# A decoder trunk on one core: seven products per weight pair in the first FFN too, with the first transposition of h behind the up projection, later weight sums, and seven raw and eleven split buffers

## The chip, the cores and the metric

The kernel runs on one core of one Trainium2 chip. The time is the device time of one execution in microseconds (us); three executions of the kernel before took 991.8 to 993.68 us, with a median of 992.76 us. One execution was taken by the hardware profiler, and all rows below come from it. Engines are named as in the profile: PE multiplies matrices, DVE is the vector engine, ACT the scalar engine, POOL the general one, and SP issues the DMAs.

## The reference

Two layers work on x, 256 tokens of 1024 channels, in float32. Each layer is a half-step SwiGLU FFN, a token mixer and a second FFN, each followed by a layer norm:

```python
def swiglu(x, w_gate, w_up, w_down):
    return (jax.nn.silu(x @ w_gate) * (x @ w_up)) @ w_down
...
for l in range(DEPTH):
    x = layer_norm(ALPHA * x + 0.5 * swiglu(x, ffn1_gate[l], ffn1_up[l], ffn1_down[l]), ...)
    # three mixers on x @ w_in[l] (short convolution, gated MLP, sparse attention), then w_out[l]
    x = layer_norm(ALPHA * x + mix, ...)
    x = layer_norm(ALPHA * x + 0.5 * swiglu(x, ffn2_gate[l], ffn2_up[l], ffn2_down[l]), ...)
```

An FFN has 2816 hidden channels: gate and up are 1024 x 2816, down is 2816 x 1024. There are four FFNs; below they are called FFN 1 to 4 in order of time, with the mixer of layer 0 between FFN 1 and FFN 2 and that of layer 1 between FFN 3 and FFN 4.

## The kernel before

Weights arrive in DRAM order as blocks of 128 x 1024 floats (512 KB) through one stream of DMAs on SP, into a pool of raw buffers. Every block is split into two parts of a shorter float format: ACT casts raw to `hi`, DVE computes `lo` = raw - hi, and a product of two split operands is three matmuls (hi*hi, lo*hi, hi*lo: `mm3`, L246 to L250, and `proj_chan`, L258 to L260). A raw buffer comes free when both parts are made; `hi` and `lo` come free when PE has used them. There are 5 raw, 12 hi and 12 lo buffers.

An FFN (`ffn`, L390) goes through the hidden channels in ten chunks, the first of 512, the others of 256. In the first chunk the tokens are the stationary side: PE makes gate and up of token half 0 and then of half 1 (`tok`; tiles pg, pu, each 24 matmuls of 512 columns). `gated` is the Silu on ACT (tile sg), `product` multiplies on DVE (tile h), and `trans` transposes h on PE (tile tr), from where it is split to hTh and hTl. The two halves use the same two PSUM banks in turn (`gu_bank`): the gate of half 1 takes the bank of the gate of half 0, and the up projection of half 1 takes the bank of the up projection of half 0, which the product h of half 0 reads. Only in FFN 1 do the gates lie in other banks, so that there the two up projections have a bank each. In the chunks after that the weights are the stationary side (`chan`, 48 matmuls of 256 columns for gate and as many for up).

The down projection of the first six chunks is done in two ways. `_paired` gives 0 for FFN 1: there `down` multiplies every block of 128 hidden channels with both token halves and both halves of the output, 4 products of three matmuls of 512 columns. In the other three FFNs two blocks form a pair and a scheme of seven products in place of eight is used (`paired`, tiles M1 to M7). It has its price on ACT and DVE: `pair_operands` makes sums of the pair's raw weights in place (L202, four of 128 x 512 a pair) and splits them, `left_sums` does the same with h (tile S), and `combine` adds the seven results to x. The split of two of the weight sums is a closure, `rest`, that waits in `put_off` until more blocks were loaded. A pair's two raw buffers are held until `rest` has run. Seven pairs fall into the first six chunks. During these chunks gate and up of one chunk share a single bank (tag `free`), so the up projection cannot start before the Silu has read the gate. The bank `held` is kept for M3.

The framework orders the instructions of each engine itself, from the program's order, priorities and its own estimate of times; each engine then works strictly in that order. `ensure` puts loads and splits 7 blocks ahead of their use.

Of the kernel before, what the change touches and what calls it, by code (L numbers as in the profile page):

```python
# [31 lines left out]

def _paired(l, f):

    return 0 if (l, f) == (0, 1) else 6


def _w_in_groups():  # L40
# [92 lines left out]
def _build(tc, A, out):  # L133
# [3 lines left out]
    with ExitStack() as es:  # L137
        pool = lambda name, bufs, **k: es.enter_context(tc.tile_pool(name=name, bufs=bufs, **k))
        cst = pool("cst", 1)
        rawp = pool("raw", 5)  # L140
        hip = pool("hi", 12)
        lop = pool("lo", 12)
        wk = pool("wk", 9)
        sm = pool("sm", 3)
        lnp = pool("lnp", 1)
# [3 lines left out]
        def gu_bank(shape, name):  # L149
            turns.append(1)  # L150
            return ps.tile(shape, F32, name=name, tag=f"gu{len(turns) % 2}", bufs=1)
# [9 lines left out]
        loaded = []  # L161
# [3 lines left out]
        put_off = []  # L165

        def ensure(i):
            while len(loaded) <= min(i, len(plan) - 1):
                key, k, n, split, o = plan[len(loaded)]
                src = A["ws"][o:o + 128 * n].rearrange("(p c) -> p c", p=128)  # L170
                if len(key) == 4 and key[2] == "d" and key[3] < _paired(*key[:2]):
                    raw = rawp.tile([128, n], F32, name="raw", tag="raw")
                    stream.append(SP.dma_start(raw, src))
                    if k % 2 == 0:
                        loaded.append(raw)
                    else:
                        loaded[-1], rest = pair_operands(loaded[-1], raw)
                        loaded.append(loaded[-1])
                        put_off.append((len(loaded), rest))
                    continue  # L180
                if not split:
                    raw = (hip, lop)[k % 2].tile([128, n], F32, name="w1", tag=("hi", "lo")[k % 2])
                    SP.dma_start(raw, src)
                    loaded.append((raw, None))
                    continue
                raw = rawp.tile([128, n], F32, name="raw", tag="raw")
                stream.append(SP.dma_start(raw, src))
                hi = hip.tile([128, n], F32R, name="hi", tag="hi")
                lo = lop.tile([128, n], F32R, name="lo", tag="lo")
                splits.append((ACT.copy(hi, raw),  # L190
                               DVE.tensor_tensor(lo, raw, hi.bitcast(F32), ALU.subtract)))  # L191
                loaded.append((hi, lo))
                while put_off and put_off[0][0] < len(loaded) - 1:
                    put_off.pop(0)[1]()

        def pair_operands(ra, rb):
# [39 lines left out]
        def kslices(key, n, ahead=None):  # L236

            res = []
            for hi, lo in blocks(key, ahead):
                m = hi.shape[1] // n  # L240
                res += [(hi[:, i * n:(i + 1) * n], lo[:, i * n:(i + 1) * n]) for i in range(m)]
            return res
# [3 lines left out]
        def mm3(o, a, b, start, stop):  # L246

            PE.matmul(o, lhsT=a[0], rhs=b[0], start=start, stop=False)  # L248
            PE.matmul(o, lhsT=a[0], rhs=b[1], start=False, stop=False)  # L249
            return PE.matmul(o, lhsT=a[1], rhs=b[0], start=False, stop=stop)  # L250
# [34 lines left out]
        def xT(t, k):  # L285
            c = slice(t * 128, t * 128 + 128)
            return xTh[:, k, c], xTl[:, k, c]
# [101 lines left out]

        def ffn(l, f, lni, last=False, mid=None):  # L390
            n = len(CHUNKS)
            paired_chunks = _paired(l, f)
            late = 4
            y = {}
            started = set()
# [2 lines left out]
            def tok(name, t, in_y=False, ahead=None):  # L398

                w = kslices((l, f, name, 0), 512, ahead)  # L400
                if in_y:
                    p = ps.tile([128, 512], F32, name="p" + name, tag="y", bufs=4)
                else:
                    p = gu_bank([128, 512], "p" + name)
                products[:] = [mm3(p, xT(t, k), w[k], k == 0, k == KC - 1) for k in range(KC)]
                return p
# [17 lines left out]
            def product(p, sg):  # L424
                h = wk.tile([128, 512], F32, name="h", tag="w")
                DVE.tensor_tensor(h, p.rearrange("p a b -> p (a b)") if len(p.shape) == 3 else p, sg, ALU.mult)  # L426
                return h
# [3 lines left out]
            def hpair():  # L431
                return (wk.tile([128, 512], F32R, name="hTh", tag="a"),
                        wk.tile([128, 512], F32R, name="hTl", tag="a"))

            def trans(h, t):
                tr = ps.tile([128, 512], F32, name="tr", tag="tr")
                for i in range(4):
                    c = slice(i * 128, i * 128 + 128)
                    PE.transpose(tr[:, c], h[:, c], ident)
                hT[0, t] = hpair()  # L440
                if paired_chunks:
                    hf[t] = wk.tile([128, 4, 128], F32, name="hf", tag="w")
                    ACT.copy(hf[t].rearrange("p a b -> p (a b)"), tr)
                    tr = hf[t].rearrange("p a b -> p (a b)")
                split_to(*hT[0, t], tr)
# [30 lines left out]
            def paired(c, ms):  # L476

                for m in ms:
                    if m not in M:
                        tag, bufs = {3: (held, 1), 6: ("tr", 2), 7: ("tr", 2)}.get(m, ("y", 4))  # L480
                        M[m] = ps.tile([128, 512], F32, name=f"M{m}", tag=tag, bufs=bufs)
                    for i in range(CHUNKS[c][1] // 256):
                        w = blocks((l, f, "d", c))[2 * i]
                        mm3(M[m], left_side(c, i, m), w[m], c == 0 and i == 0,
                            c == paired_chunks - 1 and i == CHUNKS[c][1] // 256 - 1)
# [36 lines left out]
            h = {}  # L522
            if l == 0 and f == 1:
                sg = [gated(tok("g", 0, True, ahead=0))]
                with ExitStack() as order:
                    for i in second_x(products):
                        order.enter_context(tc.issue_after(i.ins))
                    ensure(index[l, f, "g", 0][-1] + 3)
                sg.append(gated(tok("g", 1, True)))
                h = {t: product(tok("u", t), sg[t]) for t in range(2)}  # L530
                trans(h[0], 0)
            else:
                for t in range(2):
                    sg = gated(tok("g", t))
                    if t == 1:
                        trans(h[0], 0)
                    h[t] = product(tok("u", t), sg)

            if paired_chunks:
                turns.append(1)  # L540
                free, held = f"gu{len(turns) % 2}", f"gu{1 - len(turns) % 2}"
            for c in range(1, n):
                p = chan("g", c)
                with tc.high_priority(offset=60):
                    sg = gated(p)
                if c == 1:
                    trans(h[1], 1)
                if c <= paired_chunks:
                    if c == 1:
                        for i in range(2):  # L550
                            a = lambda t, b: hf[t][:, 2 * i + b, :]
                            left_sums(0, i, a(0, 0), a(0, 1), a(1, 0), a(1, 1))
                    paired(c - 1, (1, 2, 4, 5))
                elif not paired_chunks:
                    if c > 1 and c - 2 < n - late:
                        down([c - 2], 1)
                    if c - 1 < n - late:
                        down([c - 1], 0)
                pu = chan("u", c)
                with tc.high_priority(offset=60):  # L560
                    hc = product(pu, sg)
                if c <= paired_chunks:
                    paired(c - 1, (6, 7, 3))
                hT[c] = hpair()
                split_to(*hT[c], hc)
                if c < paired_chunks:
                    a = lambda t, b: hc[:, b * 256 + t * 128:b * 256 + t * 128 + 128]
                    left_sums(c, 0, a(0, 0), a(0, 1), a(1, 0), a(1, 1))
                if c == paired_chunks:
                    combine()  # L570
                if c == 2:
                    with tc.issue_after(stream[-1].ins):
                        gb = load_ln(l, lni)
                if c == 4 and mid:
                    with tc.issue_after(stream[-1].ins):
                        mid()
# [362 lines left out]
```

## Time and profile before

| | us |
|---|---|
| median of three executions | 992.76 |
| lowest, highest | 991.8, 993.68 |
| the profiled execution | 994.34 |
| its span, first to last instruction | 992.6 |
| PE, DVE, ACT busy | 969.1, 734.8, 512.3 |

The span is a little shorter than the execution, since launch and end lie outside it. Busy shares are taken over the whole span. Because the ends of matmuls are modelled, PE's pace is read from start to start of neighbouring matmuls rather than from its busy time.

### The profile page before, as it was taken

What the parts mean: (1) busy time and instruction counts of PE and PEld (TensorE: products, weight loads), DVE (VectorE), ACT (ScalarE), POOL (GpSimd) and SP (SyncE); (2) the same over time, 40 slices, a digit from 0 to 9 for tenths busy, and PEclk for the clock granted to TensorE, in tenths of its full rate; (3) what the DMA queues carried; (4) which work ended last, traced back from release to release, by engine and by line L of the source; (5) the groups of instructions that cost most, each with busy time, mean ns of one, the idle gap of its engine ahead of it and who ended that gap; (6) DMA issues with size and microseconds to landing.
All of it is one profiled execution on the core that took longest, in us unless ns stands there. A gap on an engine that the chain in (4) does not pass through costs nothing.

```text
span 992.6 us, 16879 instructions
## 1 busy us (share of the span) xinstructions
PE 969.1 (98%) x6765; PEld 875.8 (88%) x6765; DVE 734.8 (74%) x1094; ACT 512.3 (52%) x730; POOL 19.8 (2%) x42
## 2 busy tenths in 40 slices
PE   7999999999999999999999999999999999999996
PEld 5899999899878799999879899998988778989995
DVE  5755454586869978877598888848678797888844
ACT  6644444256556655555255556534475555556520
POOL 1000000010000000000000000000000000000000
PEclk9999999999999999999999999999999999999999
DMA  7977566284323557677245667764742245757611
GB/s 256 344 237 226 181 194 193 96 324 147 111 86 128 179 180 236 194 253 233 86 151 171 233 214 253 237 200 148 256 149 80 84 158 170 253 196 232 213 60 43
DMA packets 53069, 183.19 MB, mean 185 GB/s; under 512 B 6656, under 2 KB 7168, under 8 KB 52992
## 3 DMA queue, kind: packets, MB, share of 16 engines
q1 hardware_dynamic: 52992, 182.12, 55.0%
q8 instruction: 53, 0.87, 0.4%
q14 instruction: 24, 0.20, 0.1%
HBM read 181.05 MB, written 1.05 MB: 183 GB/s over the span
## 4 chain that ended last, share of the span: by engine, by line
PE 74%; DVE 11%; DMA 9%; issue 3%; ACT 3%; SPq 0%; DVEq 0%; ACTq 0%
DMA raw<-in_ws 8%; PE pu L258 6%; PE pu L260 6%; PE pu L259 6%; PE pg L258 5%; PE pg L260 5%; PE pg L259 5%; PE y L248 4%; PE y L250 4%; PE y L249 4%; DVE raw L202 3%; PE pc L258 3%; PE pc L260 3%; PE pc L259 3%; DVE lo L263 3%
## 5 line engine op out<-in xcount | busy, mean ns | idle before, releaser
L191 DVE TENSOR_TENSOR lo<-raw,hi 128x1024 fp32r<-128x1024 f32 (+3 forms) x284 | 336.6, 1200 | 115.2 <-ACT hi L190 113.5
L190 ACT CAST hi<-raw 128x1024 fp32r<-128x1024 f32 (+3 forms) x284 | 289.8, 1034 | 247.4 <-PE pu L259 64.7
L258 PE MATMUL pu<-xTh,hi 128*128 128x256 f32 x576 | 161.7, 281 | 3.4 <-ACT sg L421 3.4
L258 PE MATMUL pg<-xTh,hi 128*128 128x256 f32 x576 | 161.6, 281 | 0.5 <-DVE h L426 0.5
L260 PE MATMUL pu<-xTh,lo 128*128 128x256 f32 x576 | 160.9, 279 | 0.0
L260 PE MATMUL pg<-xTh,lo 128*128 128x256 f32 x576 | 160.8, 279 | 0.0
L259 PE MATMUL pu<-xTl,hi 128*128 128x256 f32 x576 | 160.8, 279 | 0.0
L259 PE MATMUL pg<-xTl,hi 128*128 128x256 f32 x576 | 160.8, 279 | 0.0
L258 PEld LDWEIGHTS pu<-xTh,hi 128*128 128x128 f32 x576 | 108.0, 188 | 7.1 <-ACT sg L421 5.9
L263 ACT CAST hi<-raw 128x1024 fp32r<-128x1024 f32 x63 | 66.2, 1052 | 90.5 <-DVE raw L202 46.5
L258 PEld LDWEIGHTS pg<-xTh,hi 128*128 128x128 f32 x576 | 108.1, 188 | 2.3 <-DVE h L426 1.2
L259 PEld LDWEIGHTS pu<-xTl,hi 128*128 128x128 f32 x576 | 107.9, 187 | 1.2
L260 PEld LDWEIGHTS pu<-xTh,lo 128*128 128x128 f32 x576 | 108.2, 188 | 0.2
L259 PEld LDWEIGHTS pg<-xTl,hi 128*128 128x128 f32 x576 | 107.9, 187 | 0.5
L260 PEld LDWEIGHTS pg<-xTh,lo 128*128 128x128 f32 x576 | 108.2, 188 | 0.0
L263 DVE TENSOR_TENSOR lo<-raw,hi 128x1024 fp32r<-128x1024 f32 x63 | 76.7, 1219 | 30.6 <-ACT hi L263 21.7
L258 PE MATMUL pc<-xTh,hi 128*128 128x256 f32 x256 | 73.0, 285 | 0.5 <-DVE kd L630 0.5
L248 PE MATMUL y<-hi,hTh 128*128 128x512 f32 x184 | 72.4, 394 | 0.0
L260 PE MATMUL pc<-xTh,lo 128*128 128x256 f32 x256 | 72.4, 283 | 0.0
L259 PE MATMUL pc<-xTl,hi 128*128 128x256 f32 x256 | 71.8, 281 | 0.0
L250 PE MATMUL y<-hi,hTl 128*128 128x512 f32 x184 | 71.8, 390 | 0.0
L249 PE MATMUL y<-lo,hTh 128*128 128x512 f32 x184 | 71.6, 389 | 0.0
(188 smaller groups left out, 1702.0 us busy)
## 6 DMA issues: line engine op xcount, KB each, us to landing
raw<-in_ws SPq DMA_DIRECT2D x312, 512.0 KB, 4.6
w<-in_ws SPq DMA_DIRECT2D x8, 512.0 KB, 6.2
lng<-in_ln SPq DMA_DIRECT2D x6, 512.0 KB, 6.8
lnb<-in_ln SPq DMA_DIRECT2D x6, 512.0 KB, 7.7
raw<-in_ws SPq DMA_DIRECT2D x8, 256.0 KB, 4.8
raw<-in_ws SPq DMA_DIRECT2D x4, 420.0 KB, 4.3
x<-in_x SPq DMA_DIRECT2D x4, 256.0 KB, 5.6
out<-x SPq DMA_DIRECT2D x4, 256.0 KB, 2.1
```

The source lines that it names most:

```text
L190: splits.append((ACT.copy(hi, raw), DVE.tensor_tensor(lo, raw, hi.bitcast(F32), ALU.subtract)))
L191: DVE.tensor_tensor(lo, raw, hi.bitcast(F32), ALU.subtract)))
L202: sub = lambda o, i, j: DVE.tensor_tensor(o, i, j, ALU.subtract)
L248: PE.matmul(o, lhsT=a[0], rhs=b[0], start=start, stop=False)
L249: PE.matmul(o, lhsT=a[0], rhs=b[1], start=False, stop=False)
L250: return PE.matmul(o, lhsT=a[1], rhs=b[0], start=False, stop=stop)
L258: PE.matmul(p[:, b, :], lhsT=hi, rhs=xTh[:, k, :], start=k == 0, stop=False)
L259: PE.matmul(p[:, b, :], lhsT=hi, rhs=xTl[:, k, :], start=False, stop=False)
L260: PE.matmul(p[:, b, :], lhsT=lo, rhs=xTh[:, k, :], start=False, stop=k == KC - 1)
L263: return ACT.copy(hi, src), DVE.tensor_tensor(lo, src, hi.bitcast(F32), ALU.subtract)
```

## The change

FFN 1 is paired as the others are, so the seven products are used in all four FFNs. In the three FFNs that had them, and now in FFN 1, the transposition of h of half 0 moves from between the gate and the up projection of half 1 to behind the up projection. (In the code of FFN 1 it always stood behind up.) The split of the weight sums is put off by one more block. M4 and M3 change places in the order of the products. The raw pool grows from 5 to 7 buffers, and the pools of hi and lo shrink from 12 to 11 each.

```diff
-def _paired(l, f):
-    return 0 if (l, f) == (0, 1) else 6
+PAIRED = 6
...
-        rawp = pool("raw", 5)
-        hip = pool("hi", 12)
-        lop = pool("lo", 12)
+        rawp = pool("raw", 7)
+        hip = pool("hi", 11)
+        lop = pool("lo", 11)
...
-                while put_off and put_off[0][0] < len(loaded) - 1:
+                while put_off and put_off[0][0] < len(loaded) - 2:
                     put_off.pop(0)[1]()
...
                 for t in range(2):
                     sg = gated(tok("g", t))
-                    if t == 1:
+                    if t == 1 and not paired_chunks:
                         trans(h[0], 0)
                     h[t] = product(tok("u", t), sg)
+                if paired_chunks:
+                    trans(h[0], 0)
...
-                    paired(c - 1, (1, 2, 4, 5))
+                    paired(c - 1, (1, 2, 3, 5))
...
-                    paired(c - 1, (6, 7, 3))
+                    paired(c - 1, (6, 7, 4))
```

The diff does not show where the framework then puts the instructions. On DVE in FFN 1, this stood between the splits of x (xTl) and the two products h of the first chunk before (in `lo<-raw,hi` the first four of the seven belong to the up projection):

```order
L263 TENSOR_TENSOR xTl<-tr,xTh 128x4x128 x2
L191 TENSOR_TENSOR lo<-raw,hi 128x1024 x7
L426 TENSOR_TENSOR h<-pu,sg 128x512
L191 TENSOR_TENSOR lo<-raw,hi 128x1024 x4
L426 TENSOR_TENSOR h<-pu,sg 128x512
```

And this is the end of the same stretch now; between the four splits of the up projection and its first row stand one more b (a half-size split), one lo and one raw (a weight sum):

```order
L261 TENSOR_TENSOR b_292<-raw,b_292 128x512
L200 TENSOR_TENSOR raw<-raw 128x512
L261 TENSOR_TENSOR lo<-raw,hi 128x1024
L200 TENSOR_TENSOR raw<-raw 128x512 x4
L189 TENSOR_TENSOR lo<-raw,hi 128x1024
L200 TENSOR_TENSOR raw<-raw 128x512
L261 TENSOR_TENSOR lo<-raw,hi 128x1024
L200 TENSOR_TENSOR raw<-raw 128x512
L261 TENSOR_TENSOR lo<-raw,hi 128x1024
L189 TENSOR_TENSOR lo<-raw,hi 128x1024 x2
L261 TENSOR_TENSOR lo<-raw,hi 128x1024 x2
L424 TENSOR_TENSOR h<-pu,sg 128x512 x2
```

The work on the two weight pairs of the first chunk now stands ahead of both h: 19 instructions between the last split of the up projection and h, of which 10 have 512 elements a partition and 9 have 1024; it was three splits of 1024.

On PE in FFN 2, this was the place of the transposition of h of half 0, between the gate (pg) and the up projection (pu) of half 1:

```order
L248 MATMUL pg<-hi,xTh 128x512
L249 MATMUL pg<-lo,xTh 128x512
L250 MATMUL pg<-hi,xTl 128x512
L439 MATMUL tr<-ident,h 128x128 x4
L248 MATMUL pu<-hi,xTh 128x512
L249 MATMUL pu<-lo,xTh 128x512
```

And this is the same place now, with the 24 matmuls of pu cut to their first three and last two:

```order
L248 MATMUL pg<-hi,xTl 128x512
L256 MATMUL pg<-xTh,hi 128x256
L246 MATMUL pu<-hi,xTh 128x512
L247 MATMUL pu<-lo,xTh 128x512
L248 MATMUL pu<-hi,xTl 128x512
...
L247 MATMUL pu<-lo,xTh 128x512
L248 MATMUL pu<-hi,xTl 128x512
L437 MATMUL tr<-ident,h 128x128 x4
L257 MATMUL pg<-xTl,hi 128x256
```

The transposition now follows pu, and one matmul of the next chunk's gate comes ahead of pu.

On DVE in FFN 3, this stood between the end of the layer norm of the second token half (x_80) and h of half 0:

```order
L380 SCALAR_TENSOR_TENSOR x_80<-x_80,rs,lnb 128x512 x2
L202 TENSOR_TENSOR raw<-raw 128x512
L263 TENSOR_TENSOR b_5425<-raw,b_5425 128x512
L263 TENSOR_TENSOR xTl<-tr,xTh 128x4x128 x2
L202 TENSOR_TENSOR raw<-raw 128x512
L263 TENSOR_TENSOR lo<-raw,hi 128x1024
L202 TENSOR_TENSOR raw<-raw 128x512 x4
L191 TENSOR_TENSOR lo<-raw,hi 128x1024
L202 TENSOR_TENSOR raw<-raw 128x512
L263 TENSOR_TENSOR lo<-raw,hi 128x1024
L202 TENSOR_TENSOR raw<-raw 128x512
L263 TENSOR_TENSOR lo<-raw,hi 128x1024
```

It is followed at once by h. Now one more lo stands right behind the layer norm, and the end of the stretch reads:

```order
L200 TENSOR_TENSOR raw<-raw 128x512 x4
L189 TENSOR_TENSOR lo<-raw,hi 128x1024
L200 TENSOR_TENSOR raw<-raw 128x512
L261 TENSOR_TENSOR lo<-raw,hi 128x1024
L200 TENSOR_TENSOR raw<-raw 128x512
L261 TENSOR_TENSOR lo<-raw,hi 128x1024
L189 TENSOR_TENSOR lo<-raw,hi 128x1024
L424 TENSOR_TENSOR h<-pu,sg 128x512
```

With the lo behind the layer norm that is six splits of 1024 ahead of h where there were four; in FFN 2 and FFN 4 the same stretch has five where there were four. The number of weight sums (raw) is the same in all of them.

## Rows read from the trace of the kernel before

**Rows 1.** Page: busy time by engine, and the granted clock in 40 slices.
```profile
PE 969.1 (98%) x6765; PEld 875.8 (88%) x6765; DVE 734.8 (74%) x1094; ACT 512.3 (52%) x730; POOL 19.8 (2%) x42
PEclk9999999999999999999999999999999999999999
```

**Rows 2.** Windows of FFN 1 and FFN 2: busy time of each engine.
```profile
core 0: us, PE busy (x) PEld busy (x) DVE busy (x) ACT busy (x) POOL busy (x), PEclk, DMA share, GB/s
8.00:198.00 190.00, 190.00 (x1252) 173.76 (x1250) 108.92 (x114) 89.89 (x104) 1.71 (x3) 1.00 0.65 214
312.00:498.00 186.00, 183.27 (x1227) 167.32 (x1226) 149.79 (x200) 98.94 (x118) 1.97 (x2) 1.00 0.59 193
```

**Rows 3.** Timeline of PE, FFN 2, 3 and 4: start, length, instruction, idle before.
```profile
329.57 0.40 PE L250 MATMUL pg<-hi,xTl 128*128 128x512 f32 x1
331.74 0.63 PE L439 MATMUL tr<-ident,h 128*128 128x128 f32 x4 [1.77 <-DVE h L426]
...
517.51 0.63 PE L439 MATMUL tr<-ident,h 128*128 128x128 f32 x4 [1.20 <-DVE h L426]
...
818.65 0.63 PE L439 MATMUL tr<-ident,h 128*128 128x128 f32 x4 [1.50 <-DVE h L426]
```

**Rows 4.** Timeline of DVE, first chunk of FFN 2 and FFN 3.
```profile
306.55 3.49 DVE L191 TENSOR_TENSOR lo<-raw,hi 128x1024 fp32r<-128x1024 f32 x3
...
509.66 2.49 DVE L202 TENSOR_TENSOR raw<-raw 128x512 f32<-128x512 f32 x4
...
516.68 0.68 DVE L426 TENSOR_TENSOR h<-pu,sg 128x512 f32<-128x512 f32 x1
```

**Rows 5.** Timeline of DVE, first chunk of FFN 1.
```profile
20.40 6.95 DVE L191 TENSOR_TENSOR lo<-raw,hi 128x1024 fp32r<-128x1024 f32 x6 [0.25 <-ACT hi L190]
...
29.70 0.68 DVE L426 TENSOR_TENSOR h<-pu,sg 128x512 f32<-128x512 f32 x1
```

**Rows 6.** Timeline of PE, end of the first chunk of FFN 1.
```profile
34.02 0.40 PE L250 MATMUL pu<-hi,xTl 128*128 128x512 f32 x1
34.26 0.60 PE L439 MATMUL tr<-ident,h 128*128 128x128 f32 x4
```

**Rows 7.** Timeline of PE, its start.
```profile
7.43 1.11 PE L280 MATMUL tr<-ident,x 128*128 128x128 f32 x4 [2.70 <-DMA x<-in_x]
8.19 0.78 PE L248 MATMUL pg<-hi,xTh 128*128 128x512 f32 x1
...
12.18 0.63 PE L248 MATMUL pg<-hi,xTh 128*128 128x512 f32 x1
12.61 0.63 PE L249 MATMUL pg<-lo,xTh 128*128 128x512 f32 x1
...
13.46 0.42 PE L248 MATMUL pg<-hi,xTh 128*128 128x512 f32 x1
```

**Rows 8.** Waits of PE in FFN 2, 3 and 4: us in total, times, longest.
```profile
PE pu L258 <- ACT sg L421: 1.0, 2, 0.5
...
PE pu L258 <- ACT sg L421: 1.4, 2, 1.2
...
PE pu L258 <- ACT sg L421: 1.0, 2, 0.7
```

**Rows 9.** Timeline of PE and ACT, chunk 3 of FFN 2 (chunks count from 0).
```profile
383.59 0.39 PE L249 MATMUL M<-lo,hTh 128*128 128x512 f32 x1
383.82 0.39 PE L250 MATMUL M<-hi,hTl 128*128 128x512 f32 x1
384.73 0.38 PE L258 MATMUL pu<-xTh,hi 128*128 128x256 f32 x1 [0.52 <-ACT sg L421]
...
376.99 1.05 ACT L263 CAST hi<-raw 128x1024 fp32r<-128x1024 f32 x1 [3.15 <-DMA raw<-in_ws]
...
383.13 1.05 ACT L263 CAST hi<-raw 128x1024 fp32r<-128x1024 f32 x1 [2.05 <-DVE raw L202]
384.09 0.58 ACT L421 ACTIVATE sg<-pg 128x512 f32<-128x512 f32 x1
```

More of the change, by code (lines that the diff above doesn't have):

```diff
@@ L170, in ensure @@
                 src = A["ws"][o:o + 128 * n].rearrange("(p c) -> p c", p=128)
-                if len(key) == 4 and key[2] == "d" and key[3] < _paired(*key[:2]):
+                if len(key) == 4 and key[2] == "d" and key[3] < PAIRED:
                     raw = rawp.tile([128, n], F32, name="raw", tag="raw")
@@ L391, in ffn @@
             n = len(CHUNKS)
-            paired_chunks = _paired(l, f)
+            paired_chunks = PAIRED
             late = 4
```

## The prediction

> **What bounds the kernel now.** I read the page first: PE is busy 98% of the span, at its upper clock level in every slice after the start [rows 1]. DVE and ACT have room on the mean, so PE's number of matmuls and the places where PE stands still decide. Second, the windows of one FFN without and one with the seven products [rows 2]: the matmul side is full in FFN 1 and DVE is busy 108.9 of 190 us there, while in FFN 2 DVE has 149.8 of 186. The seven products are paid for on DVE. Third, PE's waits: in the paired FFNs PE stops once before the transposition of h of half 0, released by h on DVE, for 1.77, 1.20 and 1.50 us [rows 3], and six times before an up projection, released by the Silu on ACT, 3.4 us together [rows 8]. FFN 1 has neither: its transposition starts 0.24 us after the last up matmul, at the normal pace [rows 6].
>
> **Fewer matmuls.** In FFN 1 the first six chunks hold 14 down blocks, that is 7 pairs. Each pair took 8 products and takes 7: 7 x 3 = 21 matmuls of 512 columns less. Start to start of two of them is 0.23 us [rows 9], so 21 x 0.23 = 4.8 us come off PE, which is full there. Term: -4.8.
>
> **The price on DVE in FFN 1's first chunk.** The order shows 19 instructions on DVE between the last split of the up projection and h, 10 of 512 elements and 9 of 1024. Four of the first kind took 2.49 us and three of the second 3.49 us, which gives 0.60 and 1.14 us from start to start [rows 4]; 10 x 0.60 + 9 x 1.14 = 16.3 us. The up splits are the first four of the six that start at 20.40 and take 6.95 us [rows 5], so they end near 24.9 and h ends near 24.9 + 16.3 + 0.7 = 41.9. PE, in order, has the transposition of h next, and would be there at 34.26 [rows 6]. It would wait 7.6 us. Before, h ran at 29.70 [rows 5] and cost nothing. The two more raw buffers can let the splits start earlier, by about one split, so I take 7.0; the bounds are 5.5 (DVE a full 2 us earlier) and 9 (weights or free split buffers late). Behind the transposition on PE is the whole of chunk 1, so nothing hides this. Term: +7.0.
>
> **The clock after that wait.** The granted clock is low only at the start: matmuls of 512 columns came 0.43 us apart until 13.46, which is the 1.2 GHz level, after PE had stood for 2.70 us, and 0.23 us apart later, the 2.4 GHz level [rows 6, 7]. The work from 8.19 to 13.46 was 5.3 us long at half pace, worth 2.6 us. No wait after the start was longer than 1.77 us before, and the clock stayed [rows 1, 3]. A wait of 7 us lies nearer to the first case, so I take one such start: +2.6, with the bounds 0 and 2.6. The Trainium skill ("TensorE: Matmul & The Clock Gate", "HAM oscillation") says that a long enough wait of PE for data throws the clock back and that the next burst starts slow; no row here shows a fall in the middle of a kernel, and by that rule the sum is this same one.
>
> **The moved transposition in FFN 2 to 4.** It is meant to take PE's 4.5 us of waits [rows 3] away. But the up projection of half 1, now next on PE, goes into the bank of the up projection of half 0, which h must have read first. So PE waits for the same instruction of DVE one place earlier, and what counts is when h runs. Between the layer norm and h, DVE has one split more in FFN 2 and 4 and two more in FFN 3, 1.14 us each, and DVE ran without a gap there before: h at 516.68 in FFN 3 ended 0.15 us before PE's transposition [rows 3, 4]. One gate matmul of 0.12 us is done in the wait. Terms: +1.0, +2.2, +1.0, together +4.2. In FFN 2 and 4 some first gate matmuls also move ahead of the end of the output projection, where they wait for x; I set that to nothing, with bounds of -1.5 and +1.5 for each. If DVE were never the last, the bound below is the whole wait gone, -4.5.
>
> **Raw buffers, later sums, M3 and M4.** The waits for the Silu are late because ACT does a weight sum's cast in front of it (383.13, waiting 2.05 us for DVE), and that is late because a block arrived late (376.99, ACT waiting 3.15 us for the DMA) [rows 9]. The raw pool of 5 was full: a pair holds two buffers until its sums are cast. Holding them for one block longer costs one of the two new buffers, the other lets a DMA start one block sooner, about a sixth of a chunk. I take all six waits as gone: 3.4 us of idle time [rows 8], plus 0.16 us each because the idle time counts from a modelled end (0.91 us from start to start against a pace of 0.23 is 0.68, where 0.52 is listed [rows 9]), so 4.4. Bounds: 0 (a cast of an up block now stands in front of the Silu too, 1 us) and -6. M3 needs the left sums and M4 a late weight sum; both are off the path, 0. One hi and lo less shorten the lead of the splits by a twelfth: 0, bounds 0 and +2. Term: -4.4.
>
> **Sum.** -4.8 + 7.0 + 2.6 + 4.2 - 4.4 = +4.6 us. On the profiled execution (994.34 us, 1.74 us over its span) that is 998.9; it was 1.6 us above the median of three, so beside the median of 992.76 I expect 997.4 us.
>
> **Rivals.**
> Faster: the raw buffers were the root of it all. With seven, loads and splits run ahead in DVE's idle time, so that the queue before h is short: the h waits of FFN 2 to 4 go (-4.5), those for the Silu too (-4.4), FFN 1 waits 7.0, the clock stays, and 4.8 are saved: -6.7, 986.1 us. For it: ACT's and DVE's waits for blocks [rows 9]. Against it: DVE has no gap before h, so earlier arrival doesn't shorten its queue. It decides if DVE is found idle before h. Chance 0.2.
> No change: the clock stays, the rest is as summed: +2.0, 994.8, and some waits a little shorter. For it: no fall in the whole trace after the start [rows 1]. Chance 0.2.
> Far slower: the waits for h in FFN 2 to 4 grow to about 3 to 4 us and the clock falls at each of them: three more times 2.6, so +12.4 and 1005.2 us. For it: the start's 2.70 us of standing still was not followed by full pace [rows 7]. Against it: PE had not run before that, and 1.77 us did nothing. The Trainium skill's rule on the clock gate (same page and section) gives this result if these waits are long enough for it; that can't be seen here. Chance 0.13.
> My forecast: 0.47, with a range of its own from 994.5 to 1000.
>
> **Range and chances.** 988 to 1004 us leaves out the fastest part of the first rival and most of the third. A change of 0.2%, 2 us, is what a measurement can tell. Faster by more: the first rival and a little of the second, 0.24. Within: most of the second and the low end of the forecast, 0.22. Slower: the rest, 0.54.
>
> **What will show it.** In FFN 1: PE standing some 7 us before the transposition of h, released by DVE's h near 41, and the granted clock at half behind it or not. The number of matmuls 21 lower. In FFN 2 to 4: the wait moved to pu of half 1 and grown by one or two splits, and no wait of pu for sg. I am wrong if h of FFN 1 runs before 36, if the waits for h are gone in the other FFNs, or if the up projections still wait for the Silu.

## The result, and the profile after

The kernel became slower: 1010.94 us (median of 4 runs, 1010.42 to 1011.79) against 993.22 us for the kernel before on the same chip. The ratio is 1.0181, 95% interval 1.0164 to 1.0199. Predicted were 997.4 us, with a range of 988 to 1004. The profiled execution took 1010.48 us, its span 1008.8 us.

The page of the kernel after, in the columns of [rows 1]:

```profile
PE 972.5 (96%) x6740; PEld 877.9 (87%) x6744; DVE 777.1 (77%) x1182; ACT 529.3 (52%) x754; POOL 30.8 (3%) x42
PEclk9899999999999999999999999999999998999998
```

PE has 25 recorded matmuls less and 21 weight loads less (6744 for 6765), as many as were forecast, and is busy longer. The row of the granted clock, all nines before, now has eights, among them slice 2, in FFN 1, and slice 34, in FFN 4. DVE carries 42 us more. Windows of the kernel after, FFN 1 first (columns as in [rows 2]), then the four stretches in which the clock was low:

```profile
8.00:202.00 194.00, 187.85 (x1232) 171.45 (x1233) 151.90 (x202) 104.87 (x128) 7.80 (x3) 0.98 0.64 212
...
37.00:43.80 6.80, 3.09 (x15) 3.12 (x16) 5.99 (x7) 1.21 (x3) 0.00 (x0) 0.50 0.97 324
340.80:344.20 3.40, 3.40 (x9) 2.63 (x9) 0.27 (x1) 1.05 (x1) 0.00 (x0) 0.50 0.81 296
528.60:531.90 3.30, 3.30 (x8) 2.65 (x9) 0.00 (x0) 0.46 (x1) 0.00 (x0) 0.50 0.87 292
832.40:839.10 6.70, 4.90 (x12) 3.85 (x13) 2.60 (x4) 1.05 (x1) 0.00 (x0) 0.50 0.65 221
```

The clock fell to 0.50, the 1.2 GHz level, once in every FFN. Each time PE was standing still for h, or had just done so. These are its waits (timeline of PE, the answers to [rows 3]; in brackets the idle time before the instruction and what ended it):

```profile
40.71 1.09 PE L437 MATMUL tr<-ident,h 128*128 128x128 f32 x4 [5.71 <-DVE h L424]
...
337.39 0.38 PE L256 MATMUL pg<-xTh,hi 128*128 128x256 f32 x1 [1.63 <-ACT sg L419]
340.29 0.50 PE L246 MATMUL pu<-hi,xTh 128*128 128x512 f32 x1 [2.52 <-DVE h L424]
...
526.64 0.38 PE L256 MATMUL pg<-xTh,hi 128*128 128x256 f32 x1 [1.68 <-ACT sg L419]
528.46 0.77 PE L246 MATMUL pu<-hi,xTh 128*128 128x512 f32 x1 [1.43 <-DVE h L424]
...
831.30 0.38 PE L256 MATMUL pg<-xTh,hi 128*128 128x256 f32 x1 [1.63 <-ACT sg L419]
834.20 0.80 PE L246 MATMUL pu<-hi,xTh 128*128 128x512 f32 x1 [2.52 <-DVE h L424]
```

In FFN 2 to 4 the wait is in two pieces, with one matmul of chunk 1's gate between them. The first piece ends with the Silu of half 1's gate (`ACT sg`), the second with h. Together they are 4.15, 3.11 and 4.15 us, where before there was one wait of 1.77, 1.20 and 1.50. (From start to start of PE's matmuls, as the expectations below count them, they are 4.6, 3.5 and 4.6, and FFN 1's is 5.9.)

On DVE the 19 instructions ahead of h in FFN 1 stand as counted, with h at 39.87 where [rows 5] had 29.70. The last four, all of 1024 elements, are the `lo` parts of two blocks and of a pair's weight sums:

```profile
35.34 2.36 DVE L189 TENSOR_TENSOR lo<-raw,hi 128x1024 fp32r<-128x1024 f32 x2
37.60 2.36 DVE L261 TENSOR_TENSOR lo<-raw,hi 128x1024 fp32r<-128x1024 f32 x2
39.87 1.29 DVE L424 TENSOR_TENSOR h<-pu,sg 128x512 f32<-128x512 f32 x2
```

For the entry to FFN 2, which the prediction set to nothing, this is DVE's timeline of the kernel after, beside [rows 4], whose three splits at 306.55 came behind the splits of token half 0 of x:

```profile
309.02 2.35 DVE L189 TENSOR_TENSOR lo<-raw,hi 128x1024 fp32r<-128x1024 f32 x2
311.30 0.69 DVE L261 TENSOR_TENSOR xTl<-tr,xTh 128x512 fp32r<-128x512 f32 x1
...
317.95 0.69 DVE L372 SCALAR_TENSOR_TENSOR x<-x,yo 128x512 f32<-128x512 f32 x1 [3.48 <-PE yo L248]
...
338.40 1.24 DVE L189 TENSOR_TENSOR lo<-raw,hi 128x1024 fp32r<-128x1024 f32 x1
339.53 0.70 DVE L424 TENSOR_TENSOR h<-pu,sg 128x512 f32<-128x512 f32 x1
```

Two of the splits stand ahead of x's own split (xTl) now. Then DVE stands 3.48 us for the output projection (yo), which comes late on PE: eight gate matmuls and one up matmul of token half 0 run ahead of its end, and the first of them waits for x. Two rows of PE's timeline:

```profile
310.70 0.50 PE L246 MATMUL pg<-hi,xTh 128*128 128x512 f32 x1 [0.64 <-ACT xTh L261]
...
314.08 0.39 PE L246 MATMUL yo<-hi,mixh 128*128 128x512 f32 x1
```

At the end of the chunk one more split, at 338.40, stands directly in front of h. And the gate of half 1 starts sooner behind the last split of x. These are that split and that gate, in the kernel before and then after:

```profile
321.56 1.28 DVE L263 TENSOR_TENSOR xTl<-tr,xTh 128x512 fp32r<-128x512 f32 x2
324.21 0.39 PE L248 MATMUL pg<-hi,xTh 128*128 128x512 f32 x1
...
328.45 1.29 DVE L261 TENSOR_TENSOR xTl<-tr,xTh 128x512 fp32r<-128x512 f32 x2
329.99 0.39 PE L246 MATMUL pg<-hi,xTh 128*128 128x512 f32 x1
```

The gate follows 0.2 us behind the end of x's split where it was 1.4, so more of DVE's work in front of h falls behind the gate, where PE waits for it.

Stage by stage, from start to start of PE's matmuls (us); e1 to e11 are the experiments below. Columns 2 to 4 add up FFN 2, 3 and 4; an "entry" runs from a mixer's first matmul to the gate of half 1; "rest" is chunk 2 to the end of each:

```
kernel   start+FFN 1   two entries   gate to up   up to chunk 1   chunk 1   rest    last matmul
before      198.0         252.3         22.9          17.1          65.2    416.8      984.4
after       202.0         256.5         29.9          23.5          65.6    411.0     1000.5
e1          196.9         257.4         32.3          22.7          65.8    411.3      998.4
e2          206.6         252.3         21.8          18.2          66.9    419.0      996.8
e3          198.4         258.7         16.8          17.9          66.0    411.0      981.0
e4          202.4         252.3         16.8          17.9          66.8    411.9      980.1
e5          198.7         256.5         29.8          18.2          65.3    411.0      991.8
e6          196.9         258.0         28.5          19.8          66.1    415.4      996.8
e7          196.0         251.7         30.2          22.7          65.0    412.0      989.6
e8          196.5         251.7         16.8          17.9          67.1    412.3      974.4
e9          197.5         252.8         17.9          17.1          68.6    418.0      983.9
e10         195.9         252.4         17.9          17.1          65.7    412.1      973.1
e11         196.4         253.3         22.0          18.2          66.3    414.8      983.0
```

FFN 3's stretch up to the gate of half 1, 12.1 to 12.3 us in all of them, is left out. Where the transposition of half 0 is moved (after, e2 to e5, e8, e11), its 0.35 us stands in "up to chunk 1", so 18.2 is full pace there, and 17.1 elsewhere. The start (the first gate matmul, at 6.7 to 8.6) moves by up to 1.9 us between profiled executions, and FFN 1 without the seven products took 188.5 to 189.9 us in eight of them, so a difference of 1 us in the second column means little. After minus before is 4.0 + 4.2 + 7.0 + 6.4 + 0.4 - 5.8 = 16.2 us (16.1 by the last matmuls, unrounded); of the 4.0, FFN 1 has 3.5 (193.3 for 189.8) and the start 0.4.

### The profile page after: what moved, and what is told of

Same layout as the page of the kernel before. It is cut to its first block, busy times and chain, and to the rows that moved or that the text cites. A ratio compares the mean times of both kernels' runs of the same rounds, so it can differ in the third digit from the quotient of the medians.

```text
span 1008.8 us, 16970 instructions
## 1 busy us (share of the span) xinstructions
PE 972.5 (96%) x6740; PEld 877.9 (87%) x6744; DVE 777.1 (77%) x1182; ACT 529.3 (52%) x754; POOL 30.8 (3%) x42
## 4 chain that ended last, share of the span: by engine, by line
PE 85%; DVE 10%; issue 2%; ACT 2%; DMA 1%; SPq 0%; DVEq 0%; ACTq 0%
PE pg L256 7%; PE pg L258 7%; PE pg L257 7%; PE pu L256 6%; PE pu L258 6%; PE pu L257 6%; PE M L246 4%; PE M L248 4%; PE M L247 4%; PE pc L258 3%; PE pc L257 3%; PE pc L256 3%; PE y L246 3%; PE y L248 3%; PE y L247 3%; DVE lo L189 2%
## 5 line engine op out<-in xcount | busy, mean ns | idle before, releaser
L188 ACT CAST hi<-raw 128x1024 fp32r<-128x1024 f32 (+2 forms) x270 | 275.1, 1035 | 261.9 <-issue 54.6
L189 DVE TENSOR_TENSOR lo<-raw,hi 128x1024 fp32r<-128x1024 f32 (+2 forms) x270 | 321.2, 1200 | 114.0 <-ACT hi L188 102.3
L261 ACT CAST hi<-raw 128x1024 fp32r<-128x1024 f32 x84 | 88.4, 1055 | 52.2 <-DVE raw L200 19.2
L261 DVE TENSOR_TENSOR lo<-raw,hi 128x1024 fp32r<-128x1024 f32 x84 | 101.8, 1224 | 10.9 <-ACT b L261 7.5
L200 DVE TENSOR_TENSOR raw<-raw 128x512 f32<-128x512 f32 x112 | 76.2, 691 | 0.2
L246 PE MATMUL M<-hi,hTh 128*128 128x512 f32 x168 | 66.8, 398 | 0.9 <-ACT hTh L261 0.7
L247 PE MATMUL M<-lo,hTh 128*128 128x512 f32 x168 | 65.3, 389 | 0.0
```

The source lines that it names most:

```text
L188: splits.append((ACT.copy(hi, raw), DVE.tensor_tensor(lo, raw, hi.bitcast(F32), ALU.subtract)))
L200: sub = lambda o, i, j: DVE.tensor_tensor(o, i, j, ALU.subtract)
L261: return ACT.copy(hi, src), DVE.tensor_tensor(lo, src, hi.bitcast(F32), ALU.subtract)
```

## The experiments

Each ratio is against the kernel before on the same chip, with its 95% interval.

### e1: the pools alone

```diff
-        rawp = pool("raw", 5)
-        hip = pool("hi", 12)
-        lop = pool("lo", 12)
+        rawp = pool("raw", 7)
+        hip = pool("hi", 11)
+        lop = pool("lo", 11)
```
(on the kernel before)

> The kernel before with only the pools changed: 7 raw and 11 split buffers. Theory P (the pools): it is the pool sizes that put DVE's and PE's instructions into another order, so most of the loss is in this edit alone. The two entries to FFN 2 and 4 cost 2.1 and 2.6 us, the longer h waits of FFN 2 to 4 about 2.4, 1.9 and 2.7 with 1.6, 1.6 and 2.3 of half-clock work behind them, less 5 us of Silu waits: about +10, 1001 to 1005 us. Theory T (the transposition and the later sums make h late, as the prediction had it): h waits stay near 1.8, 1.2 and 1.5, the entries stay, the Silu waits go: 987 to 990 us.

1007.62 us, ratio 1.0133 (1.0113 to 1.0152). Three lines of pool sizes carry most of the loss: 13.2 of 17.7 us, somewhat more than expected. The table shows the same pieces as in the whole change: entries +5.1, gate to up +9.4, up to chunk 1 +5.6, rest -5.5. Theory T falls: neither the transposition nor the sums are moved here, and h is late all the same.

### e2: the change without its pools

```diff
-        rawp = pool("raw", 7)
-        hip = pool("hi", 11)
-        lop = pool("lo", 11)
+        rawp = pool("raw", 5)
+        hip = pool("hi", 12)
+        lop = pool("lo", 12)
```
(on the changed kernel)

> The changed kernel with the pools of before: 5 raw and 12 split buffers. Theory P: DVE has 4 instructions less in front of h in FFN 1 (4 x 1.14 = 4.6 us less waiting, and the clock stays, 1.5) and one less in FFN 2 to 4 (1.1 each, and the clock stays, 1.6 to 2.3), the entries are as before (-4.7), the Silu waits come back (+4.4): about 993 to 997 us. Theory T: only the Silu waits come back: 1014 to 1016 us.

1006.15 us, ratio 1.0120 (1.0101 to 1.0138): between the theories' numbers, so each is incomplete. The entries (252.3), the stretch from gate to up (21.8) and full pace behind it (18.2) are back, as theory P has it. But FFN 1 takes 199.5 us, 9.7 more than without the seven products, and "rest" is 419.0. PE's waits in FFN 1 (total, times, longest):

```profile
PE tr L437 <- DVE h L424: 3.4, 1, 3.4
PE pg L256 <- DVE h L424: 3.3, 2, 2.1
PE M L246 <- ACT hTh L261: 3.0, 1, 3.0
```

With the old pools, PE waits less for the first h (3.4 us for 5.7) and more in the chunks behind it, and the clock fell twice in FFN 1 and once in chunk 3 of FFN 3. So the pools and the pairing of FFN 1 do not add up: the pools of 7, 11 and 11 make FFN 1's pairing cheaper and the other three FFNs dearer.

### e3 and e4: h first, with 7 and 11 and with 6 and 12 buffers

```diff
-                    h[t] = product(tok("u", t), sg)
+                    pu = tok("u", t)
+                    with tc.high_priority(offset=200):
+                        h[t] = product(pu, sg)
```
(on the changed kernel, the same in FFN 1's branch; e4 also has pools of 6, 12 and 12)

> The changed kernel with the product h of the token halves at a higher priority, so that DVE has it some 10 instructions earlier in the first chunk of each FFN. If only the place of h in DVE's queue makes the loss: the h waits (5.9 in FFN 1; 4.6, 3.5 and 4.6 in FFN 2 to 4) go with the half-clock work behind them (1.5, 1.6, 1.6, 2.3), while the entries keep their 4.7: about 985 us. Rival (DVE is full in the first chunk, the work only moves): what h gains comes back as waits of the first pair products in chunk 1 for their operands: 998 to 1004 us.

> The changed kernel with h first (as the run before it) and pools of 6 raw and 12 split buffers. Theory P: the split pools of 12 bring back the old order at the entries of FFN 2 and 4 (-4.7 against the run with 7 and 11), one raw buffer less may bring back a part of the Silu waits (+0 to +2): about 980 to 983 us. If the entries' loss has another cause (more DVE work, later sums): 984 to 988 us.

e3: 989.71 us, ratio 0.9948 (0.9929 to 0.9966). e4: 991.78 us, ratio 0.9977 (0.9963 to 0.9991). In FFN 2 to 4 DVE has h 9 to 11 instructions earlier, and the stretch from gate to up is at 16.8, without any wait, in both. The clock stays there. So that the place of h on DVE makes the waits and what follows them is shown; 21 us come back in e3 by the medians, which are of two chips, and 19.5 by the last matmuls of the table. Both sums missed all the same: e3 came between its two theories, and e4 some 9 us above the top of its own. The reason is FFN 1, and there alone the rival holds: behind the up projection of chunk 1 the pair products wait for the left sums. From that projection's start to the next product it took 8.55 us in e3 and 10.29 in e4, where its 48 matmuls take 5.66 at full pace. PE's row at the end of that wait and ACT's row in front of it in e3, then PE's row in e4:

```profile
52.39 0.59 PE L246 MATMUL M<-hi,hTh 128*128 128x512 f32 x1 [2.63 <-ACT hTh L261]
51.72 0.62 ACT L261 CAST hTh<-S 128x512 fp32r<-128x512 f32 x1 [0.99 <-DVE S L462]
...
54.50 0.80 PE L246 MATMUL M<-hi,hTh 128*128 128x512 f32 x1 [4.37 <-ACT hTh L261]
```

The windows of these stretches, e3 and then e4:

```profile
43.80:52.40 8.60, 5.93 (x49) 5.73 (x49) 8.02 (x16) 4.75 (x6) 0.00 (x0) 1.00 0.63 221
```

```profile
44.20:54.50 10.30, 5.92 (x48) 5.72 (x48) 10.17 (x20) 6.59 (x9) 0.00 (x0) 0.91 0.76 247
```

PE is idle 2.7 and 4.4 us, DVE is busy 8.02 and 10.17, and ACT waits for the sums that DVE makes (S): DVE is the bound there. Behind these waits the clock fell as well, once in each run; this is e3:

```profile
52.70:56.00 3.30, 3.30 (x9) 2.58 (x8) 2.57 (x6) 0.43 (x1) 0.00 (x0) 0.50 0.63 174
```

For the entries theory P held: 252.3 with 12 split buffers, 258.7 with 11. That e4 was no faster in sum is FFN 1 (195.3 us for 191.2).

### e5: matmuls of no use in the gaps

```diff
+            def fill(m):
+                p = ps.tile([128, 512], F32, name="fill", tag="y", bufs=4)
+                for i in range(m):
+                    PE.matmul(p, lhsT=xTh[:, i % KC, 128:256], rhs=..., start=i == 0, stop=i == m - 1)
...
                     sg = gated(tok("g", t))
+                    if t == 1:
+                        fill(14)
```
(on the changed kernel; 22 of them in front of FFN 1's transposition of h)

> The changed kernel with matmuls of no use (128x512, into a PSUM bank that nobody reads) in the gaps in which PE waits for h: 22 in FFN 1 and 14 behind the gate of half 1 in FFN 2 to 4. DVE and ACT keep their order, h is as late as before; only PE does not stand still. Theory C (the clock falls because PE stands still): the up projection of half 1 is back at 0.23 us a matmul (5.7 us where it took 7.2, 7.3 and 7.9), chunk 1's gate of FFN 1 at 5.7 for 6.8: 1.5 + 1.6 + 1.6 + 2.3 = 7 us less, about 1004 us. Rival (the slow stretches come from something else, as from the weights' transfers or DVE's use of the buffers): 1010 to 1012 us, the up projections as slow as now.

1002.27 us, ratio 1.0073 (1.0050 to 1.0096): 8.7 us less by doing more, as theory C has it. Timeline of PE in FFN 2 of e5, where h comes as late as without this edit:

```profile
332.76 3.35 PE L523 MATMUL fill<-xTh 128*128 128x512 f32 x14
...
337.45 0.50 PE L246 MATMUL pu<-hi,xTh 128*128 128x512 f32 x1 [1.11 <-DVE h L424]
```

And the 24 matmuls of that up projection, in windows, of the changed kernel first and then of e5:

```profile
340.20:347.50 7.30, 7.21 (x24) 5.72 (x25) 2.52 (x4) 3.15 (x3) 0.00 (x0) 0.77 0.67 205
```

```profile
337.40:343.10 5.70, 5.64 (x24) 4.58 (x25) 2.46 (x3) 3.16 (x3) 0.00 (x0) 1.00 0.71 211
```

The stretch from gate to up is the same in both kernels (29.9 and 29.8), and the 24 matmuls after it take 5.7 us in place of 7.2: only the pace changed, 5.3 us in three FFNs. The whole of FFN 1 is 2.1 us shorter. Another 1.1 us is the start, which has nothing to do with the edit.

### e6 and e7: each pool alone

```diff
-        hip = pool("hi", 12)
-        lop = pool("lo", 12)
+        hip = pool("hi", 11)
+        lop = pool("lo", 11)
```
(e6, on the kernel before; e7 has 12 and a raw pool of 6 for 5)

> The kernel before with only the split buffers cut from 12 to 11 (raw stays 5). Theory S (the number of split buffers sets the order of PE and DVE where the mixer ends): gate matmuls move ahead of the output projection, the stretch from the mixer's start to the gate of half 1 grows by 2.7 us in layer 0 and 2.3 in layer 1 as in the first run; h has the same place on DVE, so the h waits stay below 2 us and the clock stays: 998 to 1000 us. Rival (that order comes from the 7 raw buffers): 993 to 995 us.

> The kernel before with only one raw buffer more (6), split buffers 12. Theory R (raw buffers let weight work pass h on DVE): two splits more in front of h in FFN 2 to 4, 2.3 us each, and half-clock work of 1.6 behind them; the entries stay; some Silu waits go (-2 to -4): 1000 to 1004 us. Rival (the pools hurt only through the split buffers): 989 to 992 us.

e6: 1006.93 us, ratio 1.0118 (1.0093 to 1.0142). e7: 1000.01 us, ratio 1.0053 (1.0028 to 1.0078). Theory S was right on the entries (+5.7), theory R on the h waits (+7.3) and the slow pace (+5.6) at unchanged entries. In FFN 3 of the kernel before, h (516.68) came right behind a split of a weight sum (L263). In e7 two more splits stand between:

```profile
516.47 1.22 DVE L263 TENSOR_TENSOR lo<-raw,hi 128x1024 fp32r<-128x1024 f32 x1
517.61 1.22 DVE L191 TENSOR_TENSOR lo<-raw,hi 128x1024 fp32r<-128x1024 f32 x1
518.74 1.22 DVE L263 TENSOR_TENSOR lo<-raw,hi 128x1024 fp32r<-128x1024 f32 x1
519.88 0.69 DVE L426 TENSOR_TENSOR h<-pu,sg 128x512 f32<-128x512 f32 x1
```

But e6 was far over what was expected: its h waits grew by 5.6 us as well. In its FFN 2 and 4 as many instructions as before stand between the layer norm and h. But one weight sum (0.6 us) has moved behind x's last split, and the gate of half 1 starts 0.2 us behind that split where it was 1.4 and 1.6. PE's waits for h in e6, one row for FFN 2, one for FFN 3:

```profile
PE tr L439 <- DVE h L426: 3.5, 1, 3.5
```

```profile
PE tr L439 <- DVE h L426: 2.8, 1, 2.8
```

In e6's trace of FFN 3 a split of a block, of the kind that in the kernel before ran ahead of x's layer norm (whose first step was at 499.21 there), stands inside it:

```profile
505.79 1.20 DVE L191 TENSOR_TENSOR lo<-raw,hi 128x1024 fp32r<-128x1024 f32 x1
```

So one buffer less puts some of the same work later, between x and h: 1.1 of the 1.6 us by which PE waits longer for h there. Each of the two sizes hurts by itself, and they don't add up (+12.4 and +5.5 against +13.2 together, where the raw pool was 7; a pool of 7 with 12 split buffers was not run).

### e8: h first, 6 and 12 buffers, FFN 1 without the seven products

```diff
+def _paired(l, f):
+    return 0 if (l, f) == (0, 1) else 6
...
-            paired_chunks = PAIRED
+            paired_chunks = _paired(l, f)
```
(on e4)

> The kernel with h first and pools of 6 and 12 (the fourth run), but with FFN 1 without the seven products, as before. If seven products in FFN 1 cost more on DVE and ACT in chunk 1 than their 4.8 us on PE: FFN 1 takes 189.8 us for 195.3, so 5.5 less than the fourth run: 984 to 987 us. Rival (the chunk-1 loss is that of the earlier h, whatever is paired): 990 to 993 us.

984.35 us, ratio 0.9887 (0.9862 to 0.9912). FFN 1 takes 188.9 us for 195.3: even with h first, the waits for DVE that its seven products bring, and the clock behind them, cost more than the 4.8 us that they spare PE.

### e9, e10 and e11: what carries the gain

```diff
-                    h[t] = product(tok("u", t), sg)
+                    pu = tok("u", t)
+                    with tc.high_priority(offset=200):
+                        h[t] = product(pu, sg)
```
(e9, on the kernel before; e10 has a raw pool of 6 as well)

```diff
-                    if t == 1:
+                    if t == 1 and not paired_chunks:
                         trans(h[0], 0)
                     h[t] = product(tok("u", t), sg)
+                if paired_chunks:
+                    trans(h[0], 0)
```
(e11, on the kernel before)

> The kernel before with nothing but h of the token halves (FFN 2 to 4) at a higher priority. If h's place in DVE's queue is what PE waits for, the stretch from the gate of half 1 to its up projection goes from 7.9, 7.3 and 7.6 us to 5.6 each: 6.1 us less, the Silu waits stay: 987 to 989 us. Rival (DVE is full there and what is put behind h comes late instead): the waits reappear in chunk 1, 992 to 994 us.

> As the run before it, with 6 raw buffers for 5 (12 split buffers). With h first, a raw buffer more can no longer push h back, and its gain is left: chunks 2 to 9 of FFN 2 to 4 by 1.5, 1.9 and 1.5 us shorter as with 6 raw buffers alone: 983 to 985 us, the same as the run with h first, FFN 1 unpaired and all parts of the change, which says that the moved transposition, the later sums and M4 behind M3 are worth nothing by themselves. Rival (these parts carry the gain of 10 us of that run): 987 to 989 us.

> The kernel before with only the transposition of h of half 0 moved behind the up projection of half 1. As the prediction had it: PE waits for the same h one place earlier, at the up projection, so nothing is won or lost but for a matmul or two: 993 to 995 us, the stretch from gate to up of half 1 at 7.5 to 8. Rival (the wait is hidden behind the up projection): 989 to 990 us, that stretch at 5.6.

e9: 991.99 us, ratio 0.9987 (0.9973 to 1.0002), no difference that this measurement can tell. Here the rival was right: gate to up fell by 5.0 us, and chunk 1 and the rest rose by 4.6, as waits for the Silu and for the transposed h (two rows of FFN 2):

```profile
PE pu L258 <- ACT sg L421: 2.3, 2, 1.7
...
PE M L248 <- ACT hTh L263: 1.1, 1, 1.1
```

e10: 984.23 us, ratio 0.9907 (0.9894 to 0.9921). One raw buffer more, which alone cost 5.5 us (e7), is worth 7.8 us once h is first. It equals e8 (which has h first in FFN 1 too, with FFN 1 at 188.9 and 189.1 us), so the moved transposition, the later sums and M4 behind M3 are together worth nothing measurable. e11: 994.47 us, ratio 1.0013 (0.9997 to 1.0030): the moved transposition by itself moves the wait and leaves its length, as the prediction had it:

```profile
PE pu L248 <- DVE h L426: 4.7, 3, 1.7
```

## Why the prediction was wrong

It had the sign and most of the places, and missed the time by 13.5 us (+17.7 measured, +4.6 forecast). Three steps of its sum failed, all in FFN 2 to 4: the clock there was taken as staying, the entries were set to nothing, and the longer wait for h was sized too small.

- **Fewer matmuls, -4.8, and the price on DVE in FFN 1, +7.0 with +2.6 for the clock.** Sum +4.8, measured +3.5 (193.3 us for 189.8). The step held: PE stood 5.7 us for h, within the bounds, and the clock fell, at half from 37.0 to 43.8, though the 48 gate matmuls and the transposition behind the wait lost 1.5 us, less than the 2.6 taken from the start. These three make 2.4; the other 1.1 of the 3.5 was not traced, and FFN 1 varies by as much between executions.
- **The moved transposition in FFN 2 to 4, +4.2.** This step was sized too small. The gate-to-up stretch grew by 7.0 us, and by 7.7 when the transposition's own time, which left it (1.1), and the gate matmul that came in (0.4) are counted. For FFN 3 the prediction's two splits (+2.2) were right: +1.9, or +2.1 so counted. In FFN 2 and 4 it took one split (+1.0 each), and the stretch grew by 2.4 and 2.7. One weight sum (0.6) more stands behind x's last split, which a count from the layer norm on does not show, and the gate of half 1 starts 1.1 and 1.4 us sooner behind that split, so that more of DVE's queue is left for PE to wait for. The working took the growth from the splits in the order, though its heading names the transposition; e11 shows that this edit by itself does nothing, e1, e6 and e7 that the pools make that order.
- **The clock in FFN 2 to 4, taken as staying.** This is the largest step that failed. The clock fell in each, 5.3 us in sum (23.5 for 18.2); e5 shows that standing still was the cause. Rival "far slower" named just this, and had a chance of 0.13. The waits it asked for, 3 to 4 us, came (3.1 to 4.2). The argument against it, that 1.77 us did nothing, said nothing of 3 or 4. The prediction's own terms made the wait of FFN 3 3.4 us (1.20 + 2.2); 3.11 came, and the clock fell there too, so the step failed by itself and not only by the size of the waits. The Trainium skill ("TensorE: Matmul & The Clock Gate", "HAM oscillation") says that a long enough wait starts the next burst slow; the rows of the changed kernel agree. In the other runs the length of a single wait does not sort the falls (last section).
- **The entry to FFN 2 and 4, set to nothing within 1.5 each.** Measured +1.8 and +2.4, both beyond the bound. The order had shown gate matmuls ahead of the output projection's end; they stood in front of its end, one of them waited for x, and x's second half came late (rows above). e6 shows that 11 split buffers make that order.
- **Raw buffers, -4.4.** Held: no wait for the Silu is left at the up projections of chunks 1 to 9, and rest and chunk 1 together are 5.4 us shorter; in e7 one raw buffer alone makes them 5.0 shorter. The first rival's idea, that the same buffers shorten the queue in front of h, is the opposite of what happened: loads that can run ahead are split ahead, and pass h.
- **M4 behind M3, 0, and the later sums.** Nothing in e8 against e10 contradicts it. Neither was run alone.

One reading of the prediction is not borne out: it calls the granted clock low at the start, but the profile's clock is 1.00 there, and only the pace of 0.43 us shows the lower level:

```profile
8.00:13.40 5.40, 5.40 (x15) 4.30 (x14) 3.92 (x7) 3.62 (x7) 0.00 (x0) 1.00 0.76 248
```

The terms that failed are 9.2 (h and clock in FFN 2 to 4) and 4.2 (entries) short, those of FFN 1 and of the raw buffers 1.3 and 1.0 too dear; with 0.4 of the start this is the 11.5 us between the sum, +4.6, and the 16.1 between the profiled executions (their medians differ by 17.7).

What stays open: FFN 1's pairing costs 9.7 us with pools of 5, 12 and 12 (e2 against before) and 3.4 with 7, 11 and 11 (after against e1). This was seen in its waits, and not taken apart further.

## What to carry to other kernels

A pool's size is a scheduling decision: compare the order of each engine's instructions for it alone, and count what a deeper pool lets pass in front of the one small instruction that another engine waits for. Give that instruction priority first, then deepen the pool: here the first alone made no measurable difference (e9), the second alone lost 5.5 us (e7), and both together won 9.6 (e10). Price a wait of PE by what follows too: each of the four falls of the clock in the changed kernel cost 1.5 to 2.2 us on top of the wait.

## What the runs showed of the hardware

- In FFN 3 of the changed kernel PE stood 1.68 and 1.43 us with one matmul of 256 columns between, and was then granted 0.50. One wait of 2.8 us (e6, FFN 3) left the clock at 1.00, while waits of 3.5 us in the same run were followed by up projections of 7.2 and 6.9 us for 5.7. The windows of the three in e6, the middle one without a fall:

```profile
334.90:342.20 7.30, 7.30 (x28) 5.84 (x26) 4.45 (x5) 4.97 (x7) 0.00 (x0) 0.77 0.69 205
524.20:530.00 5.80, 5.80 (x28) 4.69 (x27) 4.54 (x5) 4.81 (x7) 0.00 (x0) 1.00 0.85 231
830.70:837.70 7.00, 7.00 (x28) 5.59 (x27) 3.98 (x5) 4.36 (x5) 0.00 (x0) 0.80 0.54 174
```

- The length of a single wait does not sort the falls: 2.63 us in e3 (above) and 2.12 us in FFN 1 of e2 were followed by 0.50, while 2.8 us in e6 and 3.05 us in FFN 1 of e2 left 1.00. The two waits of e2, and the windows behind them:

```profile
56.91 0.50 PE L246 MATMUL M<-hi,hTh 128*128 128x512 f32 x1 [3.05 <-ACT hTh L261]
82.27 0.38 PE L256 MATMUL pg<-xTh,hi 128*128 128x256 f32 x1 [2.12 <-DVE h L424]
...
56.90:63.70 6.80, 6.79 (x30) 5.64 (x31) 6.63 (x12) 4.46 (x6) 0.00 (x0) 1.00 0.70 220
82.80:86.20 3.40, 3.40 (x18) 3.40 (x17) 3.40 (x9) 2.48 (x4) 0.00 (x0) 0.50 0.00 0
```

  What does sort them, no run here shows.

- The price of one such fall in the changed kernel was 1.5 us of lost pace in FFN 1, 2 and 3 and 2.2 in FFN 4, and in e5 matmuls whose result nobody reads bought it back.
